# Scores of a gated recurrence in groups of 32 keys, and a redivided memory between attention and gates

## The chip, the cores and the metric

The kernel runs on one core of a Trainium2 chip. The metric is device time in microseconds (us), the median of several executions of the whole program; lower is better. A core has five engines that run their own instruction streams: TensorE (PE, with its weight loads shown apart as PEld), VectorE (DVE), ScalarE (ACT), GpSimd (POOL) and SyncE (SP), which here only starts transfers. They wait for one another through semaphores.

## The reference

One layer of a bidirectional encoder over 1024 tokens of width 1024 and 16 learned meta tokens: a normalization, one wide input projection, two branches (neighbourhood attention on a 64-wide grid, and a gated linear recurrence run in both directions), gates that mix the branches, and a feed-forward part. All is float32. What matters for the change is the recurrence and the projection of the gates:

```python
a = rms_norm(h, norm_mix[l])
(q_na, k_na, v_na, q_hg, z_f, z_b, i_hg, g_hg, gate_na, gate_hg) = split_cols(a @ w_in[l])
...
# chunk_scan, forward; the backward direction runs it on reversed sequences
b = jnp.cumsum(gi, axis=-2)
A = jnp.einsum('bhtk,bhsk,bhtsk->bhts', qi, ki, jnp.exp(diff))   # s <= t, diff = b_t - b_s
o_intra = jnp.einsum('bhts,bhsv->bhtv', A, vi)
S_new = (jnp.exp(b_last[..., 0, :])[..., None] * S
         + jnp.einsum('bhsk,bhsv->bhkv', ki * jnp.exp(b_last - b), vi))
...
mix = jax.nn.sigmoid(gate_na) * y_na + jax.nn.sigmoid(gate_hg) * y_hg
```

The recurrence has 4 heads, each with keys and values of width 128. The score of a query t and a key s carries, per key channel, the product of all forget gates between the two.

## The kernel before, in words

The program is traced with a tile framework: the code names tiles in pools of on-chip memory, and the framework puts in the semaphores and orders each engine's instructions by a cost model of its own, with the order of the code as priority. Matmuls of later parts can so stand between those of earlier ones, when the model finds their inputs ready. Pools opened on the left or the right side of memory take the space that closed pools left, and a new tile waits for the last reader of the tiles it lies over.

**Projections.** `proj_steps` (L198) multiplies a block of 128 output columns with the normalized input. Operands are split in a high and a low part, and `mm3` (L133 to L135) does three matmuls per 128 rows of the contraction, so 24 per piece of 256, 272 or 512 tokens.

**Recurrence** (`hgrn`, L288 to L480; one call per head). Tokens are cut into 8 chunks of 128. Within a chunk the scores of all 128 keys against all 128 queries are put together by levels. The diagonal (L358 to L365) multiplies the sum of forward and backward keys `kd` with the plain queries. Level `lv` has a half size h = 2^lv, from 1 to 64. It gives the scores between the two halves of each block of 2h tokens: a query in one half sees a key in the other half, forward or backward by which comes first. `X` holds the keys, decayed to the border between the halves, and `QQ` the queries of both directions, decayed from that border; the access pattern of the moving operand at L375 picks the right direction for each half. Each level's matmuls are full 128 by 128 products, 8 of them, four to a PSUM bank (`sc`, pool "a", three banks). A masked copy on VectorE (L402) takes from them into `A` the cells that belong to the level, by the mask `lmask_sb` (for level l, those cells where key and query differ first in bit l). Then `X`, `Y` and `QQ` are decayed one level further (L383 to L386, L401), and the next level begins. Between a level's matmuls and its evacuation, `between` (L348) issues a piece of a projection, for this head's values or the next head's gates, so that TensorE has work while VectorE prepares the next level. After the seven levels `A` is multiplied with the values, and chunk states join the chunks (L430 to L460).

**Attention** (L506 to L652), in four pairs of heads: projections, then masked scores (`scores`, L584), exponentials, transposes and products with the values (`values`, L604). `NB` holds mask and bias of a pair; it is filled by two transfers and six subtractions on POOL. `block_sums` (L226) makes sums and differences of quarters of the normalized input and sends them to DRAM (`tsp`). A pair's result `OT` is sent to DRAM by a POOL queue transfer at L652. All of attention's tiles lie in one pool on the left.

**Gates** (L660 to L790). The gates' projection is done by a Strassen-Winograd scheme with 7 products of half blocks in place of 8. `first_gates` (L694) does two of the products for pairs of weight blocks, `gate_sums` (L736) loads a pair of raw weight blocks (`raw`), forms their sums `sx` on VectorE (`winograd`, L661 to L664) and splits them (`split`, L94 and L95), `second_operand` (L719) loads and splits a sum of inputs, and `gate_pair` (L754) does the other five products in `chain` (L670 to L672) and combines. Their tiles lie in a pool `gp` on the left, so over what attention left. Raw blocks of the input projections come from `wp`, a pool with two buffers that `load_block` (L116) shares with `gate_sums` for the even pairs.

Of the kernel before, what the change touches and what calls it, by code (L numbers as in the profile page):

```python
# [33 lines left out]
NLEV = 7  # L34
SW = P + NM
# [11 lines left out]
def layer(ctx: ExitStack, tc: tile.TileContext, x, meta, w_in, w_na, w_hg, w_o, w_up, w_dn,  # L47
# [240 lines left out]
    def hgrn(hd, hp, lmask_get, gates, more):  # L288
# [66 lines left out]

        A = hp.tile([P, 8, P], F32, tag="A", name="A")
        lmask_sb = lmask_get()
        for hf in range(2):  # L358
            tb = hf * TH
            kd = tmp("kd")  # L360
            pool.tensor_tensor(kd, X0[:, tb:tb + TH], Y[:, tb:tb + TH], op=ALU.add)
            sc = bank("a", "sc")
            for c in range(4):
                pe.matmul(sc[:, c], kd[:, c * P:(c + 1) * P], qs[hf][:, c * P:(c + 1) * P], start=True, stop=True)
            act.copy(A[:, 4 * hf:4 * hf + 4], sc)  # L365
        X, h, n = X0, 1, T
        for lv in range(NLEV):
            scs = []
            TT = TL[lv]
            for hf in range(2):  # L370
                tb = hf * TH
                sc = bank("a", "sc")
                for c in range(4):
                    pe.matmul(sc[:, c], X[:, tb + c * P:tb + (c + 1) * P],  # L374
                              fap(QQ, tb + c * P, [[2 * h, P // (2 * h)], [T + h, 2], [1, h]]),  # L375
                              start=True, stop=True)
                scs.append(sc)
# [20 lines left out]
            for hf, sc in enumerate(scs):  # L398
                tb = hf * TH
                qa = fap(QQ, tb, [[2 * h, n // 4], [T + h, 2], [1, h]])  # L400
                dve.tensor_tensor(qa, qa, fap(TT, hf * n // 2 + 1, [[2, n // 4], [n - 1, 2], [0, h]]), op=ALU.mult)  # L401
                dve.copy_predicated(A[:, 4 * hf:4 * hf + 4],  # L402
                                    lmask_sb[:, lv:lv + 1, :].broadcast_to([P, 4, P]), sc)
# [79 lines left out]
    with tc.tile_pool(name="hp", bufs=1, reuse_waits="tile") as hp:  # L483
        lm = []

        def lmask_get():
            if not lm:
                lm.append(hp.tile([P, NLEV, P], I32, name="lmask_sb"))
# [19 lines left out]
    with tc.tile_pool(name="np", bufs=1, reuse_waits="tile") as npl:  # L508
# [4 lines left out]
        V = npl.tile([P, 9, 2, P], F32R, name="Vn")  # L513
# [12 lines left out]
        for p in range(NPAIR):  # L526
            def ev_q(ps, t0, n):
# [41 lines left out]
            NB = npl.tile([P, 2, 1008], F32, tag="NB", name="NB")  # L569
            for i in range(2):  # L570
                bs = npl.tile([P, TH], F32, tag="bs", name="bs", bufs=3)[:, :384]
                sp.dma_start(bs, bias[:, (2 * p + i) * 384:(2 * p + i + 1) * 384])
                sp.dma_start(NB[:, i], wmask)
                for o, j0, m in ((0, 0, 3), (432, 1, 2), (720, 0, 2)):
                    a = NB[:, i, o:o + m * SW].rearrange("p (j c) -> p j c", c=SW)[:, :, :P]
                    pool.tensor_tensor(a, a, bs[:, j0 * P:(j0 + m) * P].rearrange("p (j c) -> p j c", c=P),
                                       op=ALU.subtract)

# [3 lines left out]
            OT = npl.tile([P, T], F32, tag="OT", name="OT")  # L582

            def scores(s, i):  # L584
# [8 lines left out]
                pr = npl.tile([P, 432], F32, tag="pr", name="pr", bufs=5)  # L593
                mn = npl.tile([P, 1], F32, tag="mn", name="mn", bufs=4)
                sm = npl.tile([P, 1], F32, tag="sm", name="sm", bufs=4)
                rc = npl.tile([P, 1], F32, tag="rc", name="rc", bufs=4)
# [7 lines left out]
            def values(s, i, js, pr):  # L604
                g, e = divmod(s, 4)
                if e == 0:
                    po[i] = [npl.tile([P, 22, P], F32R, tag=f"PT{q}", name=f"PT{q}") for q in range(2)]
# [30 lines left out]
                low = npl.tile([64, 4, P], F32, tag="low", name="low")  # L638
# [74 lines left out]
    for v in ("t1", "t3", "t4"):  # L713
# [635 lines left out]
```

## Time and profile before

| what | value |
|---|---|
| median of 3 runs | 1584.98 us (1584.27 to 1587.31) |
| profiled execution | 1584.54 us, its span 1582.8 us |
| granted TensorE clock, mean | 0.994 |
| TensorE matmul, busy | 1536.2 us, 97% of the span, 7780 records |
| TensorE weight loads, busy | 1290.8 us, 7780 records |
| VectorE, busy | 1040.3 us, 66% |
| ScalarE, busy | 641.0 us, 40% |
| POOL, busy | 399.8 us, 25% |

The span runs from the first to the last instruction of the profiled execution; its own time has 1.7 us more. Busy times of matmuls are unions of pipelined records, and each float32 matmul shows as two weight loads and two matmul records, a float32r one as one of each. A row of the groups gives line, engine, operation, output and inputs, shapes, count, then busy time and mean duration, then idle time before and who ended it. A row of the timeline gives start, duration, engine, line, and merges neighbours of one line.

### The profile page before, as it was taken

The numbers are of one execution on the slowest core, as the hardware profiler recorded it, in microseconds if no ns is written. First come the engines' busy times: TensorE is split into PE (matmuls) and PEld (weight loads), VectorE is DVE, ScalarE is ACT, GpSimd is POOL, SyncE is SP. The second block draws the span as 40 slices with busy tenths as digits, with TensorE's granted clock in tenths as the row PEclk, the third lists the DMA queues.
The fourth block names the chain that finished last, engine by engine and source line by source line (L and its number), as shares of the span: only waits on it lengthen the run. The fifth ranks groups of instructions, "written<-read, shape, count | busy, mean of one in ns | idle before, by whom it ended". The sixth has DMA issues, their size and how long they took to land.

```text
span 1582.8 us, 20654 instructions
## 1 busy us (share of the span) xinstructions
PE 1536.2 (97%) x7780; PEld 1290.8 (82%) x7780; DVE 1040.3 (66%) x1628; ACT 641.0 (40%) x1132; POOL 399.8 (25%) x359
## 2 busy tenths in 40 slices
PE   6999999998999998999999999999999999999998
PEld 5788888887888886788888887788888878887886
DVE  6666667575768866577557259666666444879566
ACT  6121121212656656534213036455555444434444
POOL 5312121212344140010000012433344300237033
PEclk9999999999999998999999999999999999999999
DMA  5101011012131223735763224444444576563324
GB/s 186 41 27 54 27 50 31 27 41 77 64 117 67 76 81 112 235 126 174 255 225 112 67 93 134 168 152 146 147 146 146 180 266 232 187 231 114 107 80 146
DMA packets 142323, 195.80 MB, mean 124 GB/s; under 512 B 8064, under 2 KB 89984, under 8 KB 142224
## 3 DMA queue, kind: packets, MB, share of 16 engines
q1 hardware_dynamic: 133856, 173.77, 33.3%
q10 hardware_dynamic: 6192, 13.37, 2.2%
q0 software_dynamic: 2176, 7.34, 1.2%
q8 instruction: 61, 1.00, 0.3%
q14 instruction: 38, 0.31, 0.1%
HBM read 139.93 MB, written 54.53 MB: 123 GB/s over the span
## 4 chain that ended last, share of the span: by engine, by line
PE 83%; DVE 9%; issue 3%; ACT 2%; DMA 2%; POOL 1%; DVEq 0%; POOLq 0%; SPq 0%; ACTq 0%
PE mm L134 10%; PE mm L133 10%; PE mm L135 10%; PE mm L1092 4%; PE pa L1092 4%; PE pb L670 4%; PE pb L672 4%; PE pb L671 4%; PE pc L1092 4%; PE sc L374 4%; PE pb L1092 4%; PE pc L672 2%; PE pc L670 2%; PE pc L671 2%; PE pa L670 2%
## 5 line engine op out<-in xcount | busy, mean ns | idle before, releaser
L133 PE MATMUL mm<-aT,hi 128*128 128x512 f32 (+2 forms) x640 | 227.9, 356 | 2.9 <-DVE QX L532 2.3
L135 PE MATMUL mm<-aT,lo 128*128 128x512 f32 (+2 forms) x640 | 226.8, 354 | 0.0
L134 PE MATMUL mm<-aT,hi 128*128 128x512 f32 (+2 forms) x640 | 226.3, 354 | 0.0
L95 DVE TENSOR_TENSOR dl<-ur,dh 128x1024 fp32r<-128x1024 f32 x55 | 76.6, 1393 | 93.3 <-ACT dh L94 93.2
L133 PEld LDWEIGHTS mm<-aT,hi 128*128 128x128 f32 x640 | 120.8, 189 | 15.9 <-issue 2.4
L135 PEld LDWEIGHTS mm<-aT,lo 128*128 128x128 f32 x640 | 120.8, 189 | 13.1
L134 PEld LDWEIGHTS mm<-aT,hi 128*128 128x128 f32 x640 | 121.0, 189 | 12.6
L94 ACT CAST dh<-ur 128x1024 fp32r<-128x1024 f32 x55 | 57.9, 1053 | 161.6 <-issue 78.1
L123 ACT CAST hi<-raw 128x1024 fp32r<-128x1024 f32 x36 | 37.8, 1050 | 116.3 <-PE mm L134 93.6
L954 ACT CAST wh<-sx 128x512 fp32r<-128x512 f32 x70 | 42.5, 618 | 95.7 <-DMA sx<-in_w_up 32.8
L955 DVE TENSOR_TENSOR wl<-sx,wh 128x512 fp32r<-128x512 f32 x70 | 51.2, 739 | 30.9 <-ACT wh L954 30.9
L124 DVE TENSOR_TENSOR lo<-raw,hi 128x1024 fp32r<-128x1024 f32 x34 | 44.6, 1312 | 33.0 <-ACT hi L123 29.2
L955 DVE TENSOR_TENSOR wl<-raw,wh 128x512 fp32r<-128x512 f32 x46 | 50.2, 1091 | 23.7 <-ACT wh L954 22.9
L374 PE MATMUL sc<-QQ,X 128*128 128x128 f32 x448 | 61.7, 288 | 1.4 <-DVE QQ L401 1.2
L374 PEld LDWEIGHTS sc<-QQ,X 128*128 128x128 f32 x448 | 58.2, 196 | 4.4 <-issue 2.0
L386 POOL TENSOR_TENSOR Y<-X,TN 128x512 f32<-128x512 f32 x20 | 33.8, 1690 | 110.6 <-DVE X L383 110.6
L1075 POOL TENSOR_TENSOR us<-u,uv 128x512 f32<-128x512 f32 x15 | 24.0, 1603 | 133.4 <-ACT uv L960 133.4
L959 ACT ACTIVATE uv<-uv 128x512 f32<-128x512 f32 x48 | 30.4, 633 | 67.4 <-DVE uv L1070 50.0
L1182 POOL TENSOR_TENSOR w<-w,tt 128x512 f32<-128x512 f32 x16 | 23.3, 1457 | 134.0 <-DVE tt L1181 118.1
L670 PE MATMUL pb<-nt,wh 128*128 128x512 f32 x128 | 51.1, 400 | 3.6 <-DVE uv L1063 2.6
L597 DVE CUSTOM_DVE_ANT_0 pr<-nsc,NB 128x432 f32<-128x432 f32 (+1 forms) x64 | 35.1, 558 | 26.7 <-PE nsc L592 26.5
L1092 PE MATMUL mm<-dl,dh 128*128 128x512 f32 x126 | 49.8, 395 | 2.1 <-DVE dl L95 2.1
(378 smaller groups left out, 4450.8 us busy)
## 6 DMA issues: line engine op xcount, KB each, us to landing
raw<-in_w_in SPq DMA_DIRECT2D x56, 512.0 KB, 3.8
ur<-usp SPq DMA_DIRECT2D x55, 512.0 KB, 3.4
raw<-in_w_up SPq DMA_DIRECT2D x16, 1024.0 KB, 5.8
usp<-us SPq DMA_DIRECT2D x60, 256.0 KB, 2.1
sg<-gsp SPq DMA_DIRECT2D x16, 512.0 KB, 5.0
w<-in_w_dn SPq DMA_DIRECT2D x16, 512.0 KB, 4.5
usp<-uv SPq DMA_DIRECT2D x30, 256.0 KB, 2.3
gsp<-gv ACTq DMA_DIRECT2D x24, 256.0 KB, 2.9
```

The lines of the kernel that those rows point to most:

```text
L94: act.copy(hi, src)
L95: dve.tensor_tensor(lo, src, hi.bitcast(F32), op=ALU.subtract)
L124: eng.tensor_tensor(lo[:, :kc], raw[:, :kc], hi[:, :kc].bitcast(F32), op=ALU.subtract)
L133: pe.matmul(ps, lh, rh, start=first, stop=False)
L134: pe.matmul(ps, lh, rl, start=False, stop=False)
L135: pe.matmul(ps, ll, rh, start=False, stop=last)
L374: pe.matmul(sc[:, c], X[:, tb + c * P:tb + (c + 1) * P], fap(QQ, tb + c * P, [[2 * h, P // (2 * h)], [T + h, 2], [1, h]]), start=True, sto ...
L670: pe.matmul(ps, lhs[0][:, c], rhs[0][:, k], start=first and k == 0, stop=False, skip_group_check=True)
L671: pe.matmul(ps, lhs[0][:, c], rhs[1][:, k], start=False, stop=False, skip_group_check=True)
L672: pe.matmul(ps, lhs[1][:, c], rhs[0][:, k], start=False, stop=k == 3, skip_group_check=True)
L955: dve.tensor_tensor(v(lo), src, v(hi).bitcast(F32), op=ALU.subtract)
L1092: pe.matmul(ps, a[n == 2][:, q, j * P:(j + 1) * P], b[n == 1][:, q], start=first and n == 0, stop=last and n == 2, skip_group_check=True)
```

## The change

In the recurrence the scores are no longer full 128 by 128 products. For the diagonal and the levels with h below 32, keys and queries of one level never leave a group of 32 tokens, so each chunk becomes four products of 32 keys by 32 queries. Each gets a tile position (0, i): its 32 keys are loaded into one quarter of TensorE's columns, and its scores go to the 32 PSUM partitions of that quarter. All 8 chunks of a level fit one bank. The scores are gathered in a compact tile `AW` of 32 columns per chunk, by masks of 32 columns, for five levels; after h = 16, four ScalarE copies put its blocks on the diagonal of `A`. The level h = 32 has 4 products per chunk of 32 keys by the 32 queries of the neighbouring group; h = 64 has 2 of 64 by 64. Both need no mask: ScalarE copies go straight into `A`.

`A`'s cells that no level writes are as before: every cell belongs to the diagonal or to one level.

Between attention and gates, attention's tiles are divided: V, OT, the probabilities, their transposes and the small ones go to a new pool on the right side, the rest stays on the left. NB's loads and subtractions go to the head of each pair, ahead of its projections. The gates' second operands and `p3` go to the right, the loads and sums of the gates stay on the left, and the even pairs' raw blocks come from `gp` now and the odd ones' from `wp`. All of the first gate products are issued ahead of the first pair's sums and the four second operands.

The diff, cut:

```diff
+KG = 32
+NCOL = 5
...
+        AW = hp.tile([P, 8, KG], F32, tag="AW", name="AW")
         lmask_sb = lmask_get()
+
+        def score_bank():
+            return bank("a", "sc").rearrange("p a b -> p (a b)")
+
+        sc = score_bank()[:, :8 * KG].rearrange("p (g q) -> p g q", q=KG)
         for hf in range(2):
             tb = hf * TH
             kd = tmp("kd")
             pool.tensor_tensor(kd, X0[:, tb:tb + TH], Y[:, tb:tb + TH], op=ALU.add)
-            sc = bank("a", "sc")
             for c in range(4):
-                pe.matmul(sc[:, c], kd[:, c * P:(c + 1) * P], qs[hf][:, c * P:(c + 1) * P], start=True, stop=True)
-            act.copy(A[:, 4 * hf:4 * hf + 4], sc)
+                for i in range(0, P, KG):
+                    t = slice(c * P + i, c * P + i + KG)
+                    pe.matmul(sc[i:i + KG, 4 * hf + c], kd[:, t], qs[hf][:, t], start=True, stop=True,
+                              tile_position=(0, i))
+        act.copy(AW, sc)
         X, h, n = X0, 1, T
         for lv in range(NLEV):
-            scs = []
             TT = TL[lv]
-            for hf in range(2):
-                tb = hf * TH
-                sc = bank("a", "sc")
-                for c in range(4):
-                    pe.matmul(sc[:, c], X[:, tb + c * P:tb + (c + 1) * P],
-                              fap(QQ, tb + c * P, [[2 * h, P // (2 * h)], [T + h, 2], [1, h]]),
-                              start=True, stop=True)
-                scs.append(sc)
+            m = max(KG, h)
+            w = KG if h < KG else h
+            sc = score_bank()[:, :8 * w].rearrange("p (g q) -> p g q", q=w)
+            for g in range(8):
+                for i in range(0, P, m):
+                    t0 = g * P + i
+                    if h < KG:
+                        q = fap(QQ, t0, [[2 * h, KG // (2 * h)], [T + h, 2], [1, h]])
+                    else:
+                        q = QQ[:, 0, t0 - h:t0] if i // h % 2 else QQ[:, 1, t0 + h:t0 + 2 * h]
+                    pe.matmul(sc[i:i + m, g], X[:, t0:t0 + m], q, start=True, stop=True, tile_position=(0, i))
             between()
...
-            for hf, sc in enumerate(scs):
-                tb = hf * TH
-                qa = fap(QQ, tb, [[2 * h, n // 4], [T + h, 2], [1, h]])
+            for hf in range(2):
+                qa = fap(QQ, hf * TH, [[2 * h, n // 4], [T + h, 2], [1, h]])
                 dve.tensor_tensor(qa, qa, fap(TT, hf * n // 2 + 1, [[2, n // 4], [n - 1, 2], [0, h]]), op=ALU.mult)
-                dve.copy_predicated(A[:, 4 * hf:4 * hf + 4],
-                                    lmask_sb[:, lv:lv + 1, :].broadcast_to([P, 4, P]), sc)
+            if h < KG:
+                dve.copy_predicated(AW, lmask_sb[:, lv:lv + 1, :].broadcast_to([P, 8, KG]), sc)
+                if 2 * h == KG:
+                    for i in range(0, P, KG):
+                        act.copy(A[i:i + KG, :, i:i + KG], AW[i:i + KG])
+            else:
+                for i in range(0, P, h):
+                    o = i - h if i // h % 2 else i + h
+                    act.copy(A[i:i + h, :, o:o + h], sc[i:i + h])
...
-                lm.append(hp.tile([P, NLEV, P], I32, name="lmask_sb"))
+                lm.append(hp.tile([P, NCOL, KG], I32, name="lmask_sb"))
...
-    with tc.tile_pool(name="np", bufs=1, reuse_waits="tile") as npl:
+
+    with (tc.tile_pool(name="npr", bufs=1, side="right", reuse_waits="tile") as npr,
+          tc.tile_pool(name="np", bufs=1, reuse_waits="tile") as npl):
...
-        V = npl.tile([P, 9, 2, P], F32R, name="Vn")
+        V = npr.tile([P, 9, 2, P], F32R, name="Vn")
...
         for p in range(NPAIR):
+            NB = npl.tile([P, 2, 1024], F32, tag="NB", name="NB")
+            for i in range(2):
+                bs = npl.tile([P, TH], F32, tag="bs", name="bs", bufs=3)[:, :384]
+                sp.dma_start(bs, bias[:, (2 * p + i) * 384:(2 * p + i + 1) * 384])
+                sp.dma_start(NB[:, i, :1008], wmask)
...
-            NB = npl.tile([P, 2, 1008], F32, tag="NB", name="NB")
...
-            OT = npl.tile([P, T], F32, tag="OT", name="OT")
+            OT = npr.tile([P, T], F32, tag="OT", name="OT")
...
-                pr = npl.tile([P, 432], F32, tag="pr", name="pr", bufs=5)
+                pr = npr.tile([P, 432], F32, tag="pr", name="pr", bufs=5)
...
-                    po[i] = [npl.tile([P, 22, P], F32R, tag=f"PT{q}", name=f"PT{q}") for q in range(2)]
+                    po[i] = [npr.tile([P, 22, P], F32R, tag=f"PT{q}", name=f"PT{q}") for q in range(2)]
...
-    for v in ("t1", "t3", "t4"):
-        aV[v] = [gp.tile([P, 4, TH], F32R, name=f"a{v}{q}") for q in range(2)]
+    gpr = gps.enter_context(tc.tile_pool(name="gpr", bufs=1, side="right", reuse_waits="tile"))
...
+            if v not in aV:
+                aV[v] = [gpr.tile([P, 4, TH], F32R, name=f"a{v}{q}") for q in range(2)]
...
-            t = (wp.tile([P, KC, P], F32, tag="raw", name="raw") if m % 2 == 0 else
+            t = (wp.tile([P, KC, P], F32, tag="raw", name="raw") if m % 2 else
                  gp.tile([P, KC, P], F32, tag="raw", name="raw", bufs=2))
...
-        p3 = g_tile("p3", TH, bufs=2)
+        p3 = gpr.tile([P, TH], F32, tag="p3", name="p3", bufs=2)
...
+    first_gates((4, 5))
+    first_gates((6, 7))
     W = gate_sums(0)
-    first_gates((4, 5))
-    for v in ("t2", "t1"):
-        second_operand(v)
-    first_gates((6, 7))
-    for v in ("t3", "t4"):
+    for v in ("t2", "t1", "t3", "t4"):
         second_operand(v)
...
-    lmask = np.stack([((xr >> l) == 1) for l in range(NLEV)], 1).astype(np.int32).reshape(P, NLEV * P)
+    xr = xr[:, :KG] ^ (np.arange(P) // KG * KG)[:, None]
+    lmask = np.stack([((xr >> l) == 1) for l in range(NCOL)], 1).astype(np.int32).reshape(P, NCOL * KG)
```

More of the change, by code (lines that the diff above doesn't have):

```diff
@@ L526, in layer @@
         for p in range(NPAIR):
+            NB = npl.tile([P, 2, 1024], F32, tag="NB", name="NB")
[3 more added lines that the diff above has]
+                sp.dma_start(NB[:, i, :1008], wmask)
+                for o, j0, m in ((0, 0, 3), (432, 1, 2), (720, 0, 2)):
+                    a = NB[:, i, o:o + m * SW].rearrange("p (j c) -> p j c", c=SW)[:, :, :P]
+                    pool.tensor_tensor(a, a, bs[:, j0 * P:(j0 + m) * P].rearrange("p (j c) -> p j c", c=P),
+                                       op=ALU.subtract)
             def ev_q(ps, t0, n):
@@ L567, in layer @@
                 dve.tensor_tensor(V[:, b:b + m, :, 64:], src, V[:, b:b + m, :, :64].bitcast(F32), op=ALU.subtract)
-            NB = npl.tile([P, 2, 1008], F32, tag="NB", name="NB")
[L570 to L577, printed above, removed]
             block_sums(p, lambda: npl.tile([P, TH], F32, tag="bs", name="rt", bufs=3))
             po = {}
-            OT = npl.tile([P, T], F32, tag="OT", name="OT")
+            OT = npr.tile([P, T], F32, tag="OT", name="OT")
             def scores(s, i):
@@ L592, in scores @@
                 pe.matmul(sc[:, :w], QX[i][:, s], kll, start=False, stop=True)
-                pr = npl.tile([P, 432], F32, tag="pr", name="pr", bufs=5)
-                mn = npl.tile([P, 1], F32, tag="mn", name="mn", bufs=4)
-                sm = npl.tile([P, 1], F32, tag="sm", name="sm", bufs=4)
-                rc = npl.tile([P, 1], F32, tag="rc", name="rc", bufs=4)
+                pr = npr.tile([P, 432], F32, tag="pr", name="pr", bufs=5)
+                mn = npr.tile([P, 1], F32, tag="mn", name="mn", bufs=4)
+                sm = npr.tile([P, 1], F32, tag="sm", name="sm", bufs=4)
+                rc = npr.tile([P, 1], F32, tag="rc", name="rc", bufs=4)
                 dve.tensor_tensor_reduce(out=pr[:, :w], in0=sc[:, :w], in1=NB[:, i, o:o + w], scale=1.0,
@@ L637, in values @@
                 pe.matmul(ov, V[:, 8, i], PL[:, 9:22:4], start=False, stop=True)
-                low = npl.tile([64, 4, P], F32, tag="low", name="low")
+                low = npr.tile([64, 4, P], F32, tag="low", name="low")
                 dve.tensor_copy(low, ov[64:])
```

## The prediction, made before the change was run

> **What bounds the kernel now.** I read the page first: the busy shares, the slices and the granted clock.
>
> ```profile
> span 1582.8 us, 20654 instructions
> PE 1536.2 (97%) x7780; PEld 1290.8 (82%) x7780; DVE 1040.3 (66%) x1628; ACT 641.0 (40%) x1132; POOL 399.8 (25%) x359
> ...
> PE   6999999998999998999999999999999999999998
> ...
> PEclk9999999999999998999999999999999999999999
> ```
>
> TensorE is busy in 97% of the span and close to full in nearly every slice; the clock dips once, in the sixteenth slice. So TensorE time that is added or saved anywhere is added to or taken from the end, unless it falls into an idle moment. Next the stretches, with one row each for the recurrence (57.5 to 385.3 us), attention, its last part with the first gate sums, the seam to the gate pairs, and the gates. The columns are the length, then busy time of PE, PEld, DVE, ACT and POOL, then the granted clock.
>
> ```profile
> 57.50:385.30 327.80, 321.07 (x2009) 285.30 (x2008) 222.62 (x397) 61.39 (x116) 71.96 (x74) 0.99 0.12 36
> 385.30:578.50 193.20, 188.91 (x1147) 163.20 (x1148) 136.17 (x337) 115.47 (x275) 74.18 (x74) 1.00 0.28 90
> 578.50:626.30 47.80, 45.42 (x243) 36.33 (x241) 36.39 (x98) 31.32 (x68) 0.54 (x1) 0.96 0.25 79
> 626.30:640.00 13.70, 9.78 (x30) 6.93 (x30) 8.27 (x11) 8.19 (x13) 0.00 (x0) 0.75 0.78 263
> 640.00:768.00 128.00, 126.09 (x550) 102.65 (x550) 84.71 (x110) 55.33 (x78) 12.25 (x8) 1.00 0.50 160
> ```
>
> The recurrence, where most of the change lies, leaves TensorE 6.7 of 327.8 us idle; VectorE is busy 222.6 us there and ScalarE 61.4. VectorE is not the bound, so what the masks save on it buys nothing by itself. The one soft place is the seam at 626 us: 9.8 busy of 13.7, at a mean clock of 0.75.
>
> **The scores, what goes.** The groups by line and shape, and one level in the timeline:
>
> ```profile
> L374 PE MATMUL sc<-QQ,X 128*128 128x128 f32 x448 | 61.7, 288 | 1.4 <-DVE QQ L401 1.2 <-DVE QQ L316 0.2
> L364 PE MATMUL sc<-q,kd 128*128 128x128 f32 x64 | 8.8, 281 | 2.5 <-DVE q L314 2.3
> ...
> 88.20 1.95 PE L374 MATMUL sc<-QQ,X 128*128 128x128 f32 x16
> 89.91 0.37 PE L133 MATMUL mm<-aT,hi 128*128 128x272 f32 x1
> ```
>
> A level has 8 products and 16 records: each float32 product is two weight loads and two passes. The 16 run in 1.95 us, of which the last one's own 0.28 us overlaps what follows: (1.95 - 0.28) / 15 = 0.111 us per record. The 448 + 64 = 512 records cost 512 x 0.111 = 57 us, all on the engine that sets the end.
>
> **The scores, what comes.** Per head the diagonal and the six levels h = 1 to 32 each become 8 x 4 products of 32 keys by 32 queries, 64 records each, 7 x 64 = 448; the level h = 64 becomes 16 products of 64 by 64, 32 records. Over four heads that is 1792 small and 128 middle records, 1920 in place of 512. A pass streams a quarter of the columns, but there are 3.75 times as many passes and loads. All hangs on the price of one small record, which the trace of before does not show. These are the nearest rows, the narrow loads of the kernel, with the matmuls between them:
>
> ```profile
> 75.44 0.40 PE L134 MATMUL mm<-aT,hi 128*128 128x512 f32 x1
> 75.67 0.27 PE L334 MATMUL vmpt<-ident,vtm 128*16 128x128 f32 x1
> 75.70 0.48 PE L135 MATMUL mm<-aT,lo 128*128 128x512 f32 x1
> ...
> 75.63 0.09 PEld L334 LDWEIGHTS vmpt<-ident,vtm 128*16 128x16 f32 x1 [0.23 <-ACT vtm L332]
> 75.67 0.19 PEld L135 LDWEIGHTS mm<-aT,lo 128*128 128x128 f32 x1
> ...
> 444.09 0.14 PEld L636 LDWEIGHTS pov<-PT,Vn 128*64 128x64 f32 x1
> 444.15 0.19 PEld L635 LDWEIGHTS pov<-PT,Vn 128*128 128x128 f32 x1
> 444.26 0.14 PEld L636 LDWEIGHTS pov<-PT,Vn 128*64 128x64 f32 x1
> ```
>
> From one load's start to the next, a load of 16 columns takes 0.04 us, one of 64 columns 0.06, one of 128 columns 0.11. Against columns that is not proportional: some 0.03 to 0.04 us stay however narrow the load is. For 32 columns the line between the first two gives 0.05 us, and I take it. The instruction stream says much the same. Where TensorE had run dry, a load and its matmul came 0.03 to 0.04 us apart:
>
> ```profile
> 441.50 0.14 PEld L612 LDWEIGHTS ppt<-ident,pr 128*128 128x128 f32 x1 [0.52 <-issue]
> 441.54 0.30 PE L612 MATMUL ppt<-ident,pr 128*128 128x128 f32 x1 [0.35 <-DVE pr L601]
> ...
> 114.45 0.14 PEld L435 LDWEIGHTS kpt<-ident,X 128*128 128x128 f32 x1
> 114.45 0.33 PE L435 MATMUL kpt<-ident,X 128*128 128x128 f32 x1
> ```
>
> At 114.45 the two stand at the same moment, since both had been waiting in the engine. So the sequencer hands over one instruction in about 0.03 us, a pair in 0.06, and only what was queued ahead goes faster. Bounds: 0.06 if nothing is queued ahead, and 0.027 (a quarter of the 0.107 that 128 columns take) if loads shrink in proportion. 1792 x 0.05 + 128 x 0.06 = 97 us, so the scores cost **+40 us**; by the upper bound 1920 x 0.06 = 115, +58; by the lower 1792 x 0.027 + 128 x 0.054 = 55, -2.
>
> The Trainium skill, TensorEngine Tiling (Array Packing), section Performance Considerations, speaks against the change: it gives every matmul an overhead of about 60 cycles, as long with one moving column as with 60, and advises not to take a tiling factor from a dimension that is already small. Here the moving side falls to 32 columns together with the stationary side. The measured 0.04 us for 16 columns agrees in kind; no row here has 32 moving columns.
>
> **Entering and leaving a quarter's mode.** The only partial tiles of before give two answers. The 64-column loads at 444 us alternate with 128-column ones without a stop, and so does the 16-column one at 75.67. The product over 16 of the 128 rows does stop:
>
> ```profile
> 355.85 0.40 PE L135 MATMUL mm<-aT,lo 128*128 128x512 f32 x1
> 356.08 0.40 PE L133 MATMUL mm<-aT,hi 128*128 128x512 f32 x1
> 356.40 0.48 PE L427 MATMUL pum<-Vm,kmT 16*128 16x128 f32 x2
> 356.82 0.50 PE L134 MATMUL mm<-aT,hi 128*128 128x512 f32 x1
> 357.16 0.40 PE L135 MATMUL mm<-aT,lo 128*128 128x512 f32 x1
> ```
>
> Without a stop the last of these would begin at 356.08 + 0.23 + 2 x 0.11 + 0.23 = 356.76; it begins 0.40 later, for one way in and one way out. The change cuts columns, not rows, so I take 0, bound 0.40 for each of 4 x 9 groups of scores (two diagonals and seven levels per head), 14 us.
>
> The same page of the Trainium skill, section Tiling Modes, says that a change of tiling mode drains the engine. The rows at 356 us agree for rows, those at 444 us do not for columns; by the rule the sum would be 14 us higher.
>
> **Masks and copies.** 56 masked copies go to 20 of half the size; 8 copies of the diagonal go to 4 halves, and 4 + 4 + 2 small copies into A per head come.
>
> ```profile
> L402 DVE COPY_PREDICATED A<-lmask_sb,sc 128x512 f32<-128x512 int32 x56 | 41.2, 736 | 10.4 <-PE sc L374 10.4
> ...
> L365 ACT COPY A<-sc x8: 586/588/588, 59.0 to 320.0; 128x512 f32<-128x512 f32 x8
> ...
> 71.52 0.41 DVE L328 COPY V<-vpt 128x256 f32<-128x256 f32 x1
> ...
> 607.09 0.35 ACT L623 CAST PT<-ppt 128x256 fp32r<-128x256 f32 x1
> ```
>
> VectorE drops from 41 us to about 20 x 0.41 = 8. ScalarE goes from 8 x 0.59 = 5 us to 4 x (9 x 0.35 + 2 x 0.59) = 17. Both lie under TensorE's 321 us, ScalarE with 61 us of work: 0. If that cover were gone the loss would be the 12 us. A level now waits for both halves of QQ (two updates of L401), but a projection's piece of 24 matmuls runs between levels, 3 to 5 us: 0. Fewer score banks are held, which frees nothing that TensorE waits for.
>
> **Attention and the gates' first sums.** NB's two loads and six subtractions on POOL stand ahead of a pair's projections now; POOL is busy 74 of 193 us there, TensorE never waits for NB: 0. The seam itself:
>
> ```profile
> 621.64 0.54 POOL L652 DMA_DIRECT2D osp<-OT  x1 [50.07 <-DVE OT L641]
> ...
> 625.89 0.39 PE L672 MATMUL mm<-aT,lo 128*128 128x512 f32 x1
> 627.37 0.69 DVE L662 TENSOR_TENSOR sx<-sx,raw 128x512 f32<-128x512 f32 x1 [4.71 <-DMA osp<-OT]
> ...
> 629.95 0.80 PE L670 MATMUL pc<-aT,hi 128*128 128x512 f32 x1 [3.67 <-ACT hi L94]
> ...
> 614.60:618.00 3.40, 2.87 (x7) 2.29 (x8) 1.27 (x4) 0.74 (x2) 0.00 (x0) 0.50 0.53 154
> 629.95:635.06 5.11, 5.07 (x11) 3.58 (x12) 4.59 (x7) 3.16 (x6) 0.00 (x0) 0.50 1.00 315
> ```
>
> The sums of the first gate block (sx) lie in OT's memory and wait for OT's store; the first chain of the gate pairs waits 3.67 us for them, and then runs 5.11 us at a clock of 0.50, which loses 2.6 more. With OT and the values' tiles on the other side, the sums need only memory that the last scores free, and four more gate blocks, 4 x 24 matmuls of 0.23 = 22 us, go ahead of the first pair. Gain 6.2, I take **-6 us**. At most the half-clock stretch at 614.6 goes too (1.7 us) with the idle before it, about 10 in all. At least 2: those 22 us have no gate pair between them now, and VectorE must do in them 4 x 1.2 (low halves of blocks) + 4 x 0.7 (sums) + 3.1 (their low halves) + 16 x 0.7 (second operands) = 22 us as well, so a wait of four conversions, 2.8 us, can come back ahead of the first pair with a dip of the clock.
>
> **Sum.** The profiled execution took 1584.54 us, 1.7 over its span and 0.4 under the median of 1584.98. 1584.5 + 40 - 6 = **1619 us**. Its own range: 0.045 per record and the full 10 give 1606, 0.06 and 2 give 1641.
>
> **Rivals.** *The load shrinks with its columns* (0.027 per record): -2 - 6, 1577 us, not slower, decided below 0.030 per record, where the scores no longer cost more than the seam gives back (1792 x 0.03 + 7.7 = 61, +4). For it: 128 and 64 columns differ by 0.05, nearly half. Against it: 16 columns still took 0.04. Chance 0.16.
>
> *Four quarters at once*: each takes its pair in 0.05 but the four overlap, 0.0125 per record, 0.03 for middle ones: 22 + 4 = 26 us, -31 - 6, 1548 us. Against it: one sequencer feeds them, and 0.03 us per instruction would have to be queued ahead. For it: nothing in this trace has neighbouring quarters to show it wrong. Chance 0.14. The Trainium skill, TensorEngine Tiling (Array Packing), section Tiling Modes, says that different tiles load and multiply in parallel; no run here shows it.
>
> *Each group pays the stop of the rows at 356 us*: +14, 1633 us, chance 0.12. *A record keeps today's pace whatever its size*: 1920 x 0.111 = 213, +156 - 6, 1735 us; the 0.06 us at 444 us speak against it, chance 0.06. The forecast holds 0.52.
>
> **Chances and range.** What a measurement here can tell from no change is 0.2%, 3.2 us. Faster: all of the four quarters and most of the proportional loads, 0.26; within 0.2%: 0.03, the edge of the proportional case; slower: the rest, 0.71. The range leaves out the four quarters and the unchanged pace (0.20): from 1565, below the proportional case with the full 10 at the seam (1573) by what two quarters at a time would give (0.025 per record, 1792 x 0.025 + 5 = 50, -7 - 10: 1568), to 1652, the stops added to most of the upper price.
>
> **What would show it.** In the profile after, 64 records of one level from first to last in 3.0 to 3.8 us where 16 took 1.95, with loads about 0.05 us apart; 2 us says that the loads shrink, 1 us that quarters overlap. The recurrence then ends near 425 us instead of 385. TensorE busy there but with pieces of projections unchanged at 0.23 us a matmul. At the seam the wait for OT's store is gone and the clock stays at 1.00. The forecast is wrong if the recurrence ends before 390 us, or if the granted clock falls during the small products.

## The result, and the profile after

The changed kernel takes 1550.11 us (median of 4 runs, 1549.51 to 1550.21), beside 1584.78 us for the kernel before on the same chip; the ratio is 0.977, with a 95% interval of 0.9757 to 0.9783. The forecast of 1619 us and its range were wrong. What happened is the rival of four quarters at once, 1548 us, to which I gave a chance of 0.14. One of the ten executions of a later run, the memory part alone, went at a granted clock of 0.85 and took 1709 us; it is left out of that run's median.

The page of the kernel after, its busy shares, slices of TensorE and granted clock:

```profile
span 1548.4 us, 23448 instructions
PE 1502.1 (97%) x9188; PEld 1253.5 (81%) x9188; DVE 1008.4 (65%) x1592; ACT 654.7 (42%) x1168; POOL 401.8 (26%) x359
...
PE   6999999999999998999999999999999999999998
...
PEclk9999999999999999999999999999999999999999
```

There are 1408 more matmul records and 34 us less of TensorE's busy time: the 1920 records that came take less than the 512 that went. To see where the time was gained I take four marks from the rows of single lines; each row gives the first and the last start of its instructions. Before: the diagonal products, the transposes that end the recurrence, the last products of attention, the products after the gates.

```profile
L364 PE MATMUL sc<-q,kd x64: 275/275/348, 57.8 to 319.7; 128*128 128x128 f32 x64
L476 PE MATMUL opt<-ident,on x32: 272/273/329, 145.8 to 381.0; 128*128 128x128 f32 x32
L637 PE MATMUL pov<-PT,Vn x16: 392/422/452, 421.7 to 619.5; 128*128 128x512 f32 x16
L133 PE MATMUL mm<-o,hi x128: 388/389/389, 764.4 to 853.7; 128*128 128x512 f32 x128
```

The same four of the kernel after:

```profile
L374 PE MATMUL sc<-q,kd x256: 189/196/218, 61.2 to 300.2; 128*32 128x32 f32 x128
L495 PE MATMUL opt<-ident,on x32: 270/272/330, 141.4 to 353.2; 128*128 128x128 f32 x32
L658 PE MATMUL pov<-PT,Vn x16: 389/419/454, 394.5 to 593.6; 128*128 128x512 f32 x16
L135 PE MATMUL mm<-o,hi x128: 389/389/505, 730.4 to 820.6; 128*128 128x512 f32 x128
```

| stretch | before, us | after, us | difference |
|---|---|---|---|
| start, to the first diagonal product | 57.8 | 61.2 | +3.4 |
| recurrence, to its last transpose | 323.2 | 292.0 | -31.2 |
| attention, to its last output product | 238.5 | 240.4 | +1.9 |
| seam and gates, to the first product after them | 144.9 | 136.8 | -8.1 |
| the rest of the span | 818.4 | 818.0 | -0.4 |

The sum is -34.4 us, the difference of the two spans. The gain lies in the two places that the change touches. Attention takes 236.8 to 240.4 us in the fourteen profiles of this document, before and after and all experiments, so its +1.9 is no finding. One level of 32-key groups and the level h = 64 in the timeline of TensorE after (start, duration, line, shape, count):

```profile
89.92 0.29 PE L137 MATMUL mm<-aT,lo 128*128 128x272 f32 x1
90.14 0.76 PE L390 MATMUL sc<-QQ,X 128*32 128x32 f32 x64
90.83 0.50 PE L135 MATMUL mm<-aT,hi 128*128 128x512 f32 x1
...
96.17 0.39 PE L137 MATMUL mm<-aT,lo 128*128 128x512 f32 x1
96.49 1.15 PE L390 MATMUL sc<-QQ,X 128*64 128x64 f32 x32
97.57 0.50 PE L135 MATMUL mm<-aT,hi 128*128 128x512 f32 x1
```

64 records stand in 0.69 us, from their first start to the next product's; 16 full ones took 1.71. The last record's own 0.20 us taken off, (0.76 - 0.20) / 63 = 0.009 us lie between the starts of two small records, and (1.15 - 0.22) / 31 = 0.030 between two of 64 columns.

The windows of the recurrence and of the seam (length, busy PE, PEld, DVE, ACT, POOL, granted clock):

```profile
57.50:385.30 327.80, 318.03 (x3576) 271.72 (x3575) 203.51 (x383) 88.73 (x182) 93.24 (x94) 0.99 0.16 49
...
593.60:640.00 46.40, 44.41 (x196) 36.16 (x195) 29.48 (x39) 22.73 (x36) 2.14 (x2) 1.00 0.67 211
```

### The profile page after: what moved, and what is told of

It is laid out like the page before. It is cut to its first block, busy times and chain, and to the rows that moved or that the text cites. A ratio compares the mean times of both kernels' runs of the same rounds, so it can differ in the third digit from the quotient of the medians.

```text
span 1548.4 us, 23448 instructions
## 1 busy us (share of the span) xinstructions
PE 1502.1 (97%) x9188; PEld 1253.5 (81%) x9188; DVE 1008.4 (65%) x1592; ACT 654.7 (42%) x1168; POOL 401.8 (26%) x359
## 4 chain that ended last, share of the span: by engine, by line
PE 83%; DVE 9%; issue 3%; ACT 2%; DMA 2%; POOL 1%; DVEq 0%; POOLq 0%; SPq 0%; ACTq 0%
PE mm L135 11%; PE mm L136 10%; PE mm L137 10%; PE mm L1112 4%; PE pa L1112 4%; PE pb L691 4%; PE pb L692 4%; PE pb L693 4%; PE pc L1112 4%; PE pb L1112 4%; PE pc L693 2%; PE pc L692 2%; PE pc L691 2%; PE pa L692 2%; PE pa L691 2%
## 5 line engine op out<-in xcount | busy, mean ns | idle before, releaser
L92 POOL TENSOR_SCALAR rtm<-ssq 128x1 f32<-128x1 f32 (+1 forms) x17 | 6.4, 376 | 180.4 <-ACT junk L924 156.0
L135 PE MATMUL mm<-o,hi 128*128 128x512 f32 x128 | 50.0, 390 | 0.6 <-DVE mix L850 0.6
```

The source lines that it names most:

```text
L135: pe.matmul(ps, lh, rh, start=first, stop=False)
```

## The experiments

Two theories stood at the start. **One**: products in different quarters of TensorE's columns run side by side, so the pace of the records comes from how many quarters take turns. **Two**: a record simply gets cheap when it is small, wherever it stands. The seam was a question of its own.

### The two parts alone

The scores and masks of the change, with attention's and the gates' tiles and order as before; against the kernel after, cut:

```diff
-        V = npr.tile([P, 9, 2, P], F32R, name="Vn")
+        V = npl.tile([P, 9, 2, P], F32R, name="Vn")
...
-            OT = npr.tile([P, T], F32, tag="OT", name="OT")
+            OT = npl.tile([P, T], F32, tag="OT", name="OT")
...
```

> The change's scores, masks and copies alone, with the memory and order of attention and gates as before. Theory (the two parts are independent, and four quarters work at once): the recurrence keeps the 31 us that it lost between its first diagonal product and its last transpose in the changed kernel's trace, so 1584.8 - 31 = 1554 us, or up to 1557 if the first 60 us again take 3 us longer. Rival (the gain needs the new memory, since the framework orders attention's matmuls differently): above 1560.

Measured: 1557.19 us (1556.63 to 1558.58), ratio 0.9818 (0.9801 to 0.9835). The recurrence takes 354.7 - 61.5 = 293.2 us, 30.0 less than before; the seam takes 144.6, as before. So the gain of the recurrence doesn't need the new memory.

The memory and order part alone, with full products, masks and levels as before; against the kernel before, cut:

```diff
-        V = npl.tile([P, 9, 2, P], F32R, name="Vn")
+        V = npr.tile([P, 9, 2, P], F32R, name="Vn")
...
-            OT = npl.tile([P, T], F32, tag="OT", name="OT")
+            OT = npr.tile([P, T], F32, tag="OT", name="OT")
...
```

> The division of memory and the order of the gates' first products alone, scores as before. Theory: the seam gives the 8 us between attention's last product with the values and the first product after the gates, so 1577 us. Rival (the seam's gain came from the lighter recurrence, which shifts what VectorE and the transfers do there): 1583 to 1585.

Measured: 1582.12 us (1577.76 to 1585.49), ratio 0.9974 (0.9961 to 0.9987), so 2 to 6 us; the expected 1577 us is missed by 5. The seam is 759.3 - 620.7 = 138.6 us, 6.3 less than before, without the lighter recurrence on which the rival put its gain; start and recurrence took 2.8 us more, so the time tells less of it. The two parts add up to the whole within what profiles of one arrangement differ by: -30 in the recurrence and -6 at the seam.

### How many quarters take turns

The same products in another order: all 8 chunks of one quarter, then the next quarter.

```diff
-            for g in range(8):
-                for i in range(0, P, m):
+            for i in range(0, P, m):
+                for g in range(8):
```

> The changed kernel with the two loops of the score products exchanged: all 8 chunks in one quarter of the columns, then the next quarter; the same products, loads and results. Theory (quarters overlap, each needs 4 x 0.009 = 0.036 us for a load and its pass): 64 records in 2.3 us, not 0.6, +1.7 us for 7 groups of 4 heads, and +1 us for each of the four levels of 64: 1550 + 52 = 1602 us. Rival (a narrow load and a short pass are simply cheap, 0.009 us, in whatever columns): 1550 us.

Two quarters taking turns, then the other two:

```diff
-            for g in range(8):
-                for i in range(0, P, m):
+            for g, i in [(g, i + j) for i in (0, 64) for g in range(8) for j in range(0, 64, m)]:
+                if True:
```

The diagonal's loops are turned in the same way in both. The level h = 64 has only two halves, which both runs do one after the other.

> The changed kernel with the score products ordered so that quarters 0 and 1 alternate over the 8 chunks and then quarters 2 and 3. Theory (quarters overlap): 0.018 us per record, 64 in 1.15 us, +0.58 us for 7 groups of 4 heads, and the levels of 64 go one half at a time, +1 us for four of them: 1570 us. Rival (cheap in whatever columns): 1550 us.

Halves in place of quarters, with twice the multiplications and half the records:

```diff
-KG = 32
-NCOL = 5
+KG = 64
+NCOL = 6
```

> The changed kernel with groups of 64 keys on halves of the columns in place of 32 on quarters, masks and compact tile twice as wide. Theory (per column tile a load and its pass take 0.036 us at 32 and 0.06 at 64; two halves overlap, so 0.03 per record): 32 records in 0.96 us, not 64 in 0.58, +0.38 us for 7 groups of 4 heads, 1561 us. Rival (the price is per record, 0.009 us, whatever the width): half the records, 1542 us.

One level of each in the timeline. One quarter at a time: 14 records that are all in the last quarter, a whole level, and the level h = 64, one half at a time:

```profile
85.40 0.63 PE L390 MATMUL sc<-QQ,X 128*32 128x32 f32 x14
89.02 1.91 PE L390 MATMUL sc<-QQ,X 128*32 128x32 f32 x64
90.86 0.39 PE L135 MATMUL mm<-aT,hi 128*128 128x272 f32 x1
...
101.58 1.90 PE L390 MATMUL sc<-QQ,X 128*64 128x64 f32 x32
103.40 0.50 PE L135 MATMUL mm<-aT,hi 128*128 128x512 f32 x1
```

Two quarters at a time:

```profile
87.46 1.11 PE L390 MATMUL sc<-QQ,X 128*32 128x32 f32 x64
88.50 0.39 PE L135 MATMUL mm<-aT,hi 128*128 128x272 f32 x1
```

Two halves taking turns:

```profile
87.21 1.15 PE L390 MATMUL sc<-QQ,X 128*64 128x64 f32 x32
88.30 0.39 PE L135 MATMUL mm<-aT,hi 128*128 128x272 f32 x1
```

Each ratio is to the kernel before on the same chip. The runs of two quarters and of two halves have two executions each.

| arrangement | median, us | ratio (95%) | a level, us | mean us between records |
|---|---|---|---|---|
| before: full products | 1584.78 | 1 | 1.71 | 0.111 |
| one quarter at a time | 1587.63 | 1.0005 (0.9987 to 1.0023) | 1.84 | (1.91 - 0.20) / 63 = 0.027 |
| two quarters | 1565.64 | 0.9869 (0.9847 to 0.9890) | 1.04 | (1.11 - 0.20) / 63 = 0.0144 |
| two halves | 1564.04 | 0.9845 (0.9825 to 0.9866) | 1.09 | (1.15 - 0.22) / 31 = 0.030 |
| after: four quarters | 1550.11 | 0.9770 (0.9757 to 0.9783) | 0.69 | 0.009 |

The order of the loops alone is worth 37 us, with the same instructions in the same number. So theory two falls. With two neighbours taking turns the mean pace doubles, with four it triples.

The 0.027 is a mean over four quarters in turn, and where one quarter ends the next already starts. Within a lone quarter the records stand (0.63 - 0.20) / 13 = 0.033 us apart. The starts of single records in the traces, which the timeline merges, agree and show the overlap directly. In a lone quarter one record follows the other after 0.032 us. With two quarters taking turns two records start in every 0.032 us, with four quarters four. In a lone half one record follows after 0.058 us, and with two halves taking turns two start in every 0.059. So a quarter keeps its own pace whether its neighbours work or not: they run side by side.

My expectation for the run of one quarter, 1602 us, was too high by 14 us: it took 0.036 us per record, where the mean was 0.027. For two quarters and for halves it held within 5 us; the rival's 1550, 1550 and 1542 us did not.

### Is it the issue of instructions or the passes?

Each score product issued twice (the second overwrites the first with the same values):

```diff
-                    pe.matmul(sc[i:i + m, g], X[:, t0:t0 + m], q, start=True, stop=True, tile_position=(0, i))
+                    for _ in range(2):
+                        pe.matmul(sc[i:i + m, g], X[:, t0:t0 + m], q, start=True, stop=True, tile_position=(0, i))
```

> The changed kernel with each score product issued twice in a row, into the same place. Theory (the engine takes these instructions as fast as they come, 0.009 us a record for however long, and twice in a row means the same quarter twice, 0.036 + 0.036 with three other quarters still overlapping only partly): 64 records more, at least +0.58 us in 7 groups of 4 heads and +0.96 in the levels of 64, 1570 us; up to 1590 if a quarter's own pairs queue up. Rival (the prediction's sequencer hands over a pair in 0.057 us, and the short bursts lived on what was queued ahead): 64 x 0.057 in 28 groups, +102 us, 1652 us.

Measured: 1582.55 us (1581.72 to 1587.99), 32 us over the kernel after for 1920 more records; this is inside the theory's 1570 to 1590 us, and far under the rival's 1652. The first level of the first head and a later one in the timeline:

```profile
65.71 1.46 PE L392 MATMUL sc<-QQ,X 128*32 128x32 f32 x89 [0.34 <-DVE QQ L318]
68.78 0.86 PE L392 MATMUL sc<-QQ,X 128*32 128x32 f32 x39 [1.61 <-issue]
...
90.14 1.48 PE L392 MATMUL sc<-QQ,X 128*32 128x32 f32 x128
91.55 0.39 PE L135 MATMUL mm<-aT,hi 128*128 128x272 f32 x1
```

The waits of TensorE in the window of the recurrence that have no releaser (total us, times, longest):

```profile
PE sc L392 <- issue: 5.8, 5, 1.8
...
PE mm L135 <- issue: 1.2, 1, 1.2
PE mm L136 <- issue: 0.7, 1, 0.7
```

(1.48 - 0.20) / 127 = 0.010 us between records, through 256 instructions on end: the sequencer's 0.03 us per instruction, on which the forecast leaned, doesn't exist for such a stream. In the profile the recurrence takes 385.5 - 58.6 = 326.9 us, 34.9 more than after, and the start 2.6 less. By its regular groups the doubled work costs 24 us: 24 levels by 1.41 - 0.69, four levels h = 64 by about 1, eight diagonal halves by 0.37. The seven stops of the last rows are 7.7 us together, and the kernel after has none in this window (below). The 3 us that are left I do not place.

The level h = 64 as quarters, 32 keys by 64 queries, 64 records in place of 32:

```diff
-            m = max(KG, h)
+            m = KG
...
-                        q = QQ[:, 0, t0 - h:t0] if i // h % 2 else QQ[:, 1, t0 + h:t0 + 2 * h]
+                        b0 = g * P + i // h * h
+                        q = QQ[:, 0, b0 - h:b0] if i // h % 2 else QQ[:, 1, b0 + h:b0 + 2 * h]
```

> The changed kernel with the level h = 64 cut into four products of 32 keys by 64 queries per chunk: 64 records in place of 32 in that level. Theory one (the pass is what a quarter waits for: 64 float32 columns take twice the 32, some 0.06 us per quarter, 0.015 per record): 0.96 us as before, 1550 us. Theory two (the load of 32 columns is what it waits for, 0.009 per record): 0.58 us, -0.4 us in each of four levels, 1548.5 us.

Measured: 1551.11 us (1547.64 to 1555.0), ratio 0.9764 (0.9739 to 0.979), no difference from the change. Its level:

```profile
98.18 1.10 PE L391 MATMUL sc<-QQ,X 128*32 128x64 f32 x64
```

(1.10 - 0.22) / 63 = 0.014 us per record, as theory one has it, against 0.009 with half the queries and the same load. For one quarter that is 4 x 0.014 = 0.056 us, and for one half in the change 2 x 0.030 = 0.060: the load half as wide, the same 64 queries, nearly the same time. So what a quarter waits for is the pass over the queries, hardly the load and not the issue; twice the records here cost nothing.

### The seam

The memory of the change, with the gates' first products and second operands in the order of before:

```diff
-    first_gates((4, 5))
-    first_gates((6, 7))
     W = gate_sums(0)
-    for v in ("t2", "t1", "t3", "t4"):
+    first_gates((4, 5))
+    for v in ("t2", "t1"):
+        second_operand(v)
+    first_gates((6, 7))
+    for v in ("t3", "t4"):
         second_operand(v)
```

> The changed kernel with the gates' first products, first sums and second operands in the order of before, memory divided as in the change. Theory (the wait for OT's store under the sums was the seam's loss, and the memory alone takes it away): 1550 to 1551 us. Rival (the first gate products ahead of the pairs are what covers the sums): +3 to +6, 1553 to 1556 us.

The other way round, the order of the change with OT on the left again:

```diff
-            OT = npr.tile([P, T], F32, tag="OT", name="OT")
+            OT = npl.tile([P, T], F32, tag="OT", name="OT")
```

> The change as it is, but the tile OT, whose store the gates' first sums waited for in the kernel before, goes back to the left pool. Theory: the seam's gain of 8 us (the span from the last output product to the first product after the gates) came from taking the sums' buffers out from under OT; with OT back about 6 us of it are lost, 1556 us, and the first product after the gates starts some 28 us earlier than before instead of 34. Rival: the gain came from the other tiles that moved, and OT's place does not matter: 1550 us.

And both edits at once:

> The change, but with the tile OT back on the left pool and with the order of the gates' first products and second operands as before; what is left of the memory part is the division of the other tiles. In the run with OT back alone the first sums ran at 601.9 us, behind OT's store, and not at 586 to 592 as in the change, yet the seam from the last output product to the first product after the gates kept 5.6 of its 8.1 us. Theory: the products of the blocks 4 to 7, moved ahead, covered the late sums there; with neither the place nor the order the sums are late and uncovered, the seam gains 2 us or less, and the time is 1555 to 1557 us. Rival: OT's store costs nothing any more, because the other tiles that moved let the loads run earlier: the seam still gains 5 to 8 us, 1550 to 1552 us.

The seam is counted from the last output product to the first product after the gates, in one profiled execution of each run; the sums are those of the first gate block. In the eight other profiles with the memory and order of the change the seam takes 134.9 to 138.9 us, so a difference of 2 us between two rows is no finding.

| OT | order | sums start, against the last output product | seam, us | against before | median, us |
|---|---|---|---|---|---|
| right | ahead (the change) | 7.3 us earlier | 136.8 | -8.1 | 1550.11 |
| right | as before | 10.6 us earlier | 137.3 | -7.6 | 1551.24 (1548.9 to 1554.71) |
| left | ahead | 11.7 us later | 139.3 | -5.6 | 1551.48 (1547.9 to 1553.71) |
| left | as before | 5.1 us later | 147.7 | +2.8 | 1562.51 (1559.37 to 1564.7) |

The first sum on VectorE in the run with OT on the left:

```profile
601.93 0.69 DVE L682 TENSOR_TENSOR sx<-raw 128x512 f32<-128x512 f32 x1 [2.81 <-DMA raw<-in_w_in]
```

The first sum and the first gate pair's products in the run with both edits, and its window from 600 us on:

```profile
596.89 0.69 DVE L682 TENSOR_TENSOR sx<-raw 128x512 f32<-128x512 f32 x1 [3.26 <-DMA raw<-in_w_in]
...
603.25 0.79 PE L691 MATMUL pc<-aT,hi 128*128 128x512 f32 x1 [4.69 <-ACT hi L96]
```

```profile
600.00:612.00 12.00, 8.75 (x29) 6.90 (x30) 7.87 (x11) 7.16 (x12) 0.00 (x0) 0.72 0.82 271
```

Either half of the edit saves the seam, and together they add little. With OT on the right the sums are done before attention ends. With OT on the left the raw blocks land late and the sums with them; in the order of the change 4 x 24 = 96 more products stand ahead of the first pair and cover it. With neither, TensorE waits 4.7 us, the mean clock from 600 to 612 us falls to 0.72, and the seam is no better than before.

With the order of before and OT on the right the time held the expected 1550 to 1551 us. My theory for the run with OT back (a loss of 6 us) was wrong: its seam of 139.3 us is 0.4 above the eight, and the median shows no loss. The theory for both edits was right that the loss comes back, and too low by 6 us. One cause that my expectations name is not shown: in these two runs the sums do not wait for OT's store but for raw blocks, whose loads were issued at 587.2 and 596.9 us (order of the change) and at 588.7 and 589.3 us (both edits), in the change at 573.3 and 580.8. With both edits that is ahead of OT's store, which was issued at 593.9 us. Why these loads are issued later with OT on the left stays open.

### The start

The change does nothing ahead of 57 us, and yet its first diagonal product came 3.4 us later. The normalization below already starts 0.6 us later; the rest comes behind it. Before, around 13.4 us, VectorE (L105) and POOL (L124):

```profile
13.35 1.29 DVE L105 SCALAR_TENSOR_TENSOR na<-xt,rs,g_bc 128x1024 f32<-128x1024 f32 x1 [0.72 <-ACT hi L123]
13.44 3.43 POOL L124 TENSOR_TENSOR lo<-raw,hi 128x1024 fp32r<-128x1024 f32 x1
```

After, the same two instructions:

```profile
13.93 2.35 POOL L126 TENSOR_TENSOR lo<-raw,hi 128x1024 fp32r<-128x1024 f32 x1
13.93 3.43 DVE L107 SCALAR_TENSOR_TENSOR na<-xt,rs,g_bc 128x1024 f32<-128x1024 f32 x1 [0.72 <-POOL rs L93]
```

They exclude each other: whoever comes second takes about 3.4 us. To take the collision away, the first block's low half goes to VectorE, and in a second run the second block's too:

```diff
-        early = {C_ZF: load_block(w_in[:, C_ZF:C_ZF + P], KC, eng=pool)}
+        early = {C_ZF: load_block(w_in[:, C_ZF:C_ZF + P], KC)}
```

> The change, with the first weight block's low half formed on VectorE instead of POOL. In all profiles so far POOL's subtraction and a normalization on VectorE start within 0.1 us of each other at 13 to 14 us, and one of the two takes 3.4 us: VectorE's in the change, POOL's in the kernel before; the first diagonal product then comes at 60 to 61.5 us or at 58 to 59. Theory: the two exclude each other, and who is held sets 2 to 3 us of the start; without POOL's subtraction neither lasts 3.4 us there, the first diagonal product comes by 59 us, and the time is 1547 to 1549 us, if VectorE's extra 1.2 us are not on the path. Rival: the start is set by the transfers, and the first diagonal product stays at 60 us or later, 1550 to 1552 us.

> As the run before, with the second early weight block's low half on VectorE too (in the change POOL takes 3.40 us for it at 28.7 us). Theory: the second collision holds POOL, which nothing on the path waits for, so this gives nothing beyond the first: within 1 us of that run. Rival: the normalizations that POOL holds up there were on the path as well, and the first diagonal product comes 1 to 2 us earlier still.

The diagonal products of the first of these runs:

```profile
L374 PE MATMUL sc<-q,kd x256: 189/196/218, 59.2 to 297.7; 128*32 128x32 f32 x128
```

They start 2.0 us earlier than in the change (expected: by 59 us), and the normalization at 14.27 us takes 1.29. With both blocks moved they start at 58.6. The times are 1548.08 us (1547.14 to 1553.04; ratio 0.9763, 0.9746 to 0.9779) and 1549.57 us (1547.91 to 1551.72; ratio 0.9765, 0.9752 to 0.9779). The second run was expected within 1 us of the first; it is 1.5 slower, inside the intervals. The mechanism is shown in the profiles; a gain over the change is not, since the intervals overlap.

## Why the prediction was wrong

**The step that failed** is the price of one small record in "The scores, what comes": 0.05 us, where the runs show 0.009. It had two parts, and both were wrong.

*What sets the price.* I read it from the spacing of narrow loads that stand between full ones, and took their remainder of 0.03 to 0.04 us as a part that stays however narrow a load is. That spacing goes with the passes, the matmul records, and not with the width of the loads. These rows of the kernel before stand beside the loads at 444 us in the prediction:

```profile
444.09 0.22 PE L635 MATMUL pov<-PT,Vn 128*128 128x128 f32 x1
444.20 0.33 PE L635 MATMUL pov<-PT,Vn 128*128 128x256 f32 x1
444.38 0.19 PEld L635 LDWEIGHTS pov<-PT,Vn 128*128 128x128 f32 x1
```

The load of 64 columns at 444.09 us stands 0.06 us ahead of the next load, beside a pass of 128 columns. The same load at 444.26 us stands 0.12 us ahead of the next, beside a pass of 256. In a row of its own kind a record goes by the columns that its pass streams: 0.032 us for 32 columns, 0.058 for 64, 0.111 for 128, so about 0.027 for every 32 columns and 0.005 that stays. The lower bound of 0.027, on which the proportional rival stood, came near the price of a lone quarter for another reason than the one it was given.

*The overlap.* Neighbouring quarters run side by side, which the trace of before could not show, and I gave it little because "one sequencer feeds them, and 0.03 us per instruction would have to be queued ahead". That reading was taken where TensorE had run dry, and its first row at 441.54 us had itself been released by VectorE; a stream that had been queued went at 0.0045 us per instruction (0.009 for a pair).

With the right price the sum holds. From typical rows: 24 levels save 1.71 - 0.69 each, four levels h = 64 save 1.71 - 1.08, four diagonals about 1.71 - 0.78, together 30.7 us; the recurrence took 31.2 less. Two smaller terms cancel: the first level of a head saved more (in the last head 2.49 us became 0.82), and the way into a group costs 0.1 us more than it did with full products. The rival of four quarters said -31 by 0.0125 and 0.03 per record. That its sum came out is in part luck: its small records were too dear by 6 us, and it left out the ways in and out, which cost about as much.

**Entering and leaving a mode** was taken as 0, with a bound of 0.40 per group. The 0.69 us of 64 records at 0.009 (0.58) leave 0.1. On the way in, 0.32 us lie between the start of the product at 96.17 us and the first record behind it, where two such products stand 0.23 apart: another 0.1. So a group costs about 0.2 us, 7 us in 36 groups, half of the bound. The rival of the stops, 1633 us, is out all the same, since it kept my price of a record.

The Trainium skill, TensorEngine Tiling (Array Packing), section Tiling Modes, says that different tiles load and multiply in parallel: 0.027, 0.0144 and 0.009 us for one, two and four quarters agree. The same page of the Trainium skill, section Performance Considerations, by which a dimension that is already small should give no tiling factor, spoke against the change, and here the measurement decides against that advice: 32 moving columns in four quarters were the fastest arrangement tried.

**Masks and copies**, costed at nothing under TensorE: right. The masked copies after:

```profile
L415 DVE COPY_PREDICATED AW<-lmask_sb,sc x20: 431/440/447, 71.7 to 324.5; 128x256 f32<-128x256 int32 x20
```

20 by 0.44 is 8.8 us, where I had worked out 8. In the first window VectorE went from 222.6 to 203.5 us and ScalarE from 61.4 to 88.7, both far under TensorE; the window's end holds some 30 us of attention now, since the recurrence ends earlier.

**The seam**, -6 with bounds 2 and 10: measured -8.1, and between -6.0 and -10.0 over the nine profiles with this memory and order. The wait for OT's store is gone and the clock stays at 1.00, as I had said it would show. That a wait for conversions "can come back ahead of the first pair" happened in small: the profile after has 1.5 and 0.5 us of it at 610 us, with no dip. I had credited both the memory and the order; the runs show that one would do.

**Left out**: the start, +3.4 in the profiled execution, most of it by a collision that falls either way.

The time of 1619 us had chance 0.52 and rested on one number from the nearest row. The rows at hand could not show whether neighbouring quarters overlap, and the range should have reached to that rival.

## What to carry to other kernels

Where small products come in numbers, send neighbouring ones to different column quarters of TensorE: with the same instructions, the order of the loops alone was worth 37 us of 1587. A price per record read from a mixed stream doesn't carry over to a stream of records of its own kind: ask first whether the load or the pass beside it sets the spacing. Nor does an issue rate carry over that was read where the engine had run dry. When two edits aim at one wait, try each alone: here either was enough, and neither was visible once the other was in place.

## What the runs showed of the hardware

**The instruction stream has a limit, further out.** With each product issued twice, TensorE stopped seven times for 0.3 to 1.8 us, 7.7 us in all, with no releaser. The row of the instruction queue on the page of the kernel after and of that run:

```profile
q8 instruction: 72, 1.18, 0.3%
```

```profile
q8 instruction: 87, 1.43, 0.4%
```

3844 more instructions came with 15 more packets of 16.4 KB, so one packet brings about 256 instructions of 64 bytes; at 0.010 us a pair these are used up in 1.3 us, and a packet took 0.9 to 1.4 us to move where the stops are. Each of the seven stops ends 1.2 to 1.6 us after such a packet had landed (the one at 68.78 us after a packet that moved from 66.50 to 67.46). That TensorE ran out of instructions there is inferred from these times, not tested by an edit. The Trainium skill, Runtime: NRT & Kernel Launch, section Instruction fetch mechanics, says that instructions come in 16 KiB blocks of 256, and that fetching them stays mostly hidden; the size agrees, and these stops were not hidden. The kernel after, with 64 small records (128 instructions) on end between other matmuls, had no such stop in the recurrence.

**VectorE and POOL exclude each other at the start.** In all ten experiments before the last two, and in before and after, one of the two instructions at 13 to 14 us took 3.4 us. Where VectorE's start is recorded 0.05 us or more ahead of POOL's, POOL is held (before, the memory part alone, the doubled scores, the order of before), and the first diagonal product comes at 57.8 to 58.9 us; in the other eight VectorE is held, and it comes at 59.8 to 61.5. Profiles of kernels that do not differ there so differ by 1 to 3.7 us, and a difference of that size at the end of two profiled executions is no verdict.
